# Layer 0 of a two-layer trunk: one forward substitution for both head groups, their inverses joined side by side, scan chunks of the groups in turn, and the output projection by token tile

## The chip, the core and the metric

The kernel runs on one core of a Trainium2 chip. The metric is the time of one execution on the device, in microseconds; what is compared is the median of several executions. The core has engines that each work through their own queue in order: PE (TensorE, the matmuls; PEld is its weight loads), DVE (VectorE), ACT (ScalarE), POOL (GpSimd), and SP, which here only issues DMAs. An instruction waits at the head of its queue until what it needs is there, and everything behind it on that engine waits too.

## What is computed

Two post-norm layers over 512 tokens of width 1024. Layer 0 mixes with a gated delta rule of six heads beside a cross-attention into 256 memory tokens, then comes an MLP of width 4096; layer 1 has sliding-window attention beside its own memory attention, then the same MLP. The part that matters here is the delta rule of layer 0:

```python
k_beta = k * beta[..., None]
L = jnp.where(strict, jnp.einsum('bhnid,bhnjd->bhnij', k_beta, k) * decay, 0.0)
rhs = jnp.concatenate([v * beta[..., None], k_beta * jnp.exp(g)[..., None]], axis=-1)
sol = lax.linalg.triangular_solve(L, rhs, left_side=True, lower=True, unit_diagonal=True)
...
def step(state, inp):
    qd, kd, uc, wc, ac, cd = inp
    v_new = uc - jnp.einsum('bhik,bhkv->bhiv', wc, state)
    out = jnp.einsum('bhik,bhkv->bhiv', qd, state) + jnp.einsum('bhij,bhjv->bhiv', ac, v_new)
    state = state * cd[..., None, None] + jnp.einsum('bhik,bhiv->bhkv', kd, v_new)
    return state, out
```

q, k and v pass a short causal convolution with SiLU first; the outputs are normed, gated by SiLU(z), joined with the memory attention and projected by w_o.

## The kernel before

Most matrix products are done in two parts: a weight tile `wr` arrives by DMA, ACT casts it to a rounded high part `wh` (L87) and DVE subtracts to get the low part `wl` (L88); three matmuls per tile then give the product. Three raw tiles and four pairs of parts are in flight in layer 0, so a new weight waits for the one four back to be used up. The six heads of the delta rule are two groups of three, and the 512 tokens are four chunks of 128, so a group has 12 units (head, chunk).

What is done in layer 0's mixer is written as a list of steps, `MIXER_ORDER`: a letter names a function, digits its arguments. `run_steps` calls them in that order; a scheduler then sets the queues of the engines, keeping to the order of the calls where operands allow and moving an instruction forward where its engine would stand. The steps are:

- `E` (`make_E1`): the decay matrices of a group, by a matmul over triangular masks (DVE and POOL build one each), DVE's mask and ACT's exponential. `g`, `k` (`group_kq`): k and q of one head: 48 matmuls, convolution (ACT one tap, DVE three: L324), SiLU, then `ak` (k with k and q), the norms, and the matrices LT (for the inverse) and INT (in the place of E).
- `i` (`inv_blocks`): the inverse of LT's diagonal 32x32 blocks. Four DMAs bring the blocks of a group's 12 units to 48 partitions (through DRAM, `dl`, then `ld`), 31 steps of forward substitution on DVE follow, a product (L420) and a subtraction (L422) each, and five DMAs bring the result back (`dx`, then the blocks of `TT`).
- `j` (`inv_join`): from these blocks to the whole 128x128 inverse. DVE transposes TT to U (L433); then small matmuls `ipp`, `ip3`, `ip2` (32x32) and, twice for six units, `iqp`, `iq2` (64x64), with ACT or DVE copying each result from PSUM for the next.
- `v` and `w`: v of one head (24 matmuls, convolution, SiLU), then its transposes (`vt`, L396) and scaling.
- `c` (`group_chunk`): one chunk of the scan for a group's three heads: transposes of k (`kt`), `ks` and `qs` with the state, DVE's subtraction R, `tr` with U, ACT's scaling to vn, `ds` for the new state and `od` for the output. `o` (`chunk_out`): the output's norm (ACT's squares, one power on POOL) and its product with the gate.
- `z` projects a third of the gate for all four token tiles; `n` (`z_norm`) applies SiLU (ACT) and the norm's weight (POOL, L625). `q` projects the memory queries; `m` (`mem0`) pushes a memory unit of a token tile: scores with exponentials, transposes (`mpt`), values (`mov`); a unit's later parts run when the next ones are pushed, and `M` flushes.
- `f` (`close_tile`) transposes a finished token tile to features (`to_feapt`), `W` loads a quarter of w_o, `p` projects a quarter for one tile, `L` is the layer norm of a tile, `X` closes the mixer's pool and opens those of the MLP.

Before, the first group's inverse is begun while the second group's heads are still projected, each group has its own substitution and its own join, the first group's four chunks come before the second's, and w_o is projected mostly after all tiles are closed. PSUM has eight banks: three for long products, five in turn for all small ones.

Of the kernel before, what the change touches and what calls it, by code (L numbers as in the profile page):

```python
# [18 lines left out]
P = 128  # L19
# [30 lines left out]
def trunk(ctx: ExitStack, tc: tile.TileContext, xT, xn, memT, wk, wq, wv, wqm, wz, wmk, wmv, wo0, wo1, up, dn,  # L50
# [24 lines left out]
    def fr(ap):  # L75
        return ap.bitcast(F32)
# [164 lines left out]

    def proj_z(zg, gates=None):

        slabs = [wload(wz[zg, kh], [P, 4, CW]) for kh in range(2)]
        c0 = zg * CW
        n = min(CW, 768 - c0)
        for t in range(NT):
# [7 lines left out]
    proj_z(2, ab)  # L255


# [45 lines left out]

    def make_E1(gi):
        E1 = dt_([P, NU, P], "E1")
        for hl in range(GH):
            h = GH * gi + hl
            ps = smt("E1")
            psv = ps.rearrange("p (c i) -> p c i", c=4)
            for i, eng in enumerate((V, G)):  # L310
                gm = dt_([P, 4, P], "y", dt=F32R)
                eng.tensor_tensor(gm, triu[:, :].unsqueeze(1).broadcast_to([P, 4, P]),
                                  fr(gsp[i])[:, h * 4:h * 4 + 4].unsqueeze(2).broadcast_to([P, 4, P]), op=ALU.mult)
                T.matmul(ps, slow, gm.rearrange("p c i -> p (c i)"), start=(i == 0), stop=(i == 1))
            dst = E1[:, hl * 4:hl * 4 + 4, :]
            V.tensor_tensor(dst, psv, mtri[:, :].unsqueeze(1).broadcast_to([P, 4, P]), op=ALU.add)
            A.activation(dst, dst, AF.Exp)
        E1s[gi] = E1

# [79 lines left out]

    Q = 4 * NU  # L400

    def inv_blocks(gi):

        LT = groups[gi]["LT"]
        dl = drp.tile([4, NU, 32, 32], F32, tag="dl", name=nm("dl"))
        for b in range(4):
            q = slice(32 * b, 32 * b + 32)
            SY.dma_start(dl[b].rearrange("u j i -> j u i"), LT[q, :, q])
        ld = dt_([Q, 32, 32], "ld", bufs=1)
        SY.dma_start(ld.rearrange("q j i -> q (j i)"), dl.rearrange("b u j i -> (b u) (j i)"))  # L410
        X = dt_([Q, 32, 32], "X", bufs=1)
        G.memset(X, 0.0)
        G.memset(X.rearrange("q i m -> q (i m)")[:, 0:1024:33], 1.0)
        tmp = dt_([Q, 256], "tmp", bufs=1)
        TT = groups[gi]["TT"] = dt_([P, NU, P], f"TT{gi}", bufs=1)
        G.memset(TT, 0.0)
        for j in range(31):
            n, m = 31 - j, j + 1
            tv = tmp[:, 0:n * m].rearrange("q (i m) -> q i m", m=m)
            V.tensor_tensor(tv, ld[:, j, j + 1:32].unsqueeze(2).broadcast_to([Q, n, m]),  # L420
                            X[:, j, 0:m].unsqueeze(1).broadcast_to([Q, n, m]), op=ALU.mult)
            V.tensor_sub(X[:, j + 1:32, 0:m], X[:, j + 1:32, 0:m], tv)  # L422
        dx = drp.tile([4, NU, 32, 32], F32, tag="dx", name=nm("dx"))
        SY.dma_start(dx.rearrange("b u i m -> (b u) (i m)"), X.rearrange("q i m -> q (i m)"))
        for b in range(4):
            q = slice(32 * b, 32 * b + 32)
            SY.dma_start(TT[q, :, q], dx[b].rearrange("u i m -> i u m"))

    def inv_join(gi):
        g = groups[gi]  # L430
        LT, TT = g["LT"], g["TT"]
        U = g["U"] = dt_([P, NU, P], "U")
        V.transpose(U.rearrange("p u i -> p (u i)"), TT.rearrange("p u i -> p (u i)"))  # L433

        b0, b1, b2, b3 = (slice(32 * b, 32 * b + 32) for b in range(4))
        pp = smt("ipp")[:, 0:NU * 32].rearrange("p (u i) -> p u i", u=NU)
        for u in range(NU):
            T.matmul(pp[b1, u, :], LT[b0, u, b1], TT[b0, u, b0], start=True, stop=True)
            T.matmul(pp[b3, u, :], LT[b2, u, b3], TT[b2, u, b2], start=True, stop=True)
        Pf = dt_([P, NU, 32], "Pf")  # L440
        A.copy(Pf[b1], pp[b1])
        V.tensor_copy(Pf[b3], pp[b3])
        p2 = smt("ip2")[:, 0:NU * 32].rearrange("p (u i) -> p u i", u=NU)
        p3 = smt("ip3")[:, 0:NU * 32].rearrange("p (u i) -> p u i", u=NU)
        for u in range(NU):
            T.matmul(p3[b1, u, :], U[b1, u, b1], Pf[b1, u, :], start=True, stop=True)
        for u in range(NU):
            T.matmul(p2[b0, u, :], Pf[b1, u, :], U[b1, u, b1], start=True, stop=True)
            T.matmul(p2[b2, u, :], Pf[b3, u, :], U[b3, u, b3], start=True, stop=True)
        V.tensor_scalar(TT[b1, :, b0], p3[b1], -1.0, None, op0=ALU.mult)  # L450
        A.activation(U[b0, :, b1], p2[b0], AF.Copy, scale=-1.0)
        V.tensor_scalar(U[b2, :, b3], p2[b2], -1.0, None, op0=ALU.mult)

        lo_, hi_ = slice(0, 64), slice(64, 128)
        for u0 in range(0, NU, 6):
            pp = smt("iqp")[:, 0:384].rearrange("p (u i) -> p u i", u=6)
            for u in range(6):
                T.matmul(pp[hi_, u, :], LT[lo_, u0 + u, hi_], TT[lo_, u0 + u, lo_], start=True, stop=True)
            P2 = dt_([P, 6, 64], "Pf")
# [282 lines left out]
    def second_pools():  # L742
# [6 lines left out]


    steps = {"E": make_E1, "g": group_open, "k": group_kq, "i": inv_blocks, "j": inv_join, "v": group_v,
             "w": group_v2, "c": group_chunk, "o": chunk_out, "q": proj_qm, "m": mem0, "M": flush, "z": proj_z,
             "n": z_norm, "W": wo_open, "f": close_tile, "p": wo_tile, "X": second_pools, "L": ln_tile}
# [528 lines left out]
```

## Time and profile before

| | us |
|---|---|
| median of 3 executions | 1174.53 (1172.65 to 1175.73) |
| the profiled execution | 1170.9 |
| its span, first to last instruction | 1169.2 |
| PE busy | 1137.7 (97%) |
| DVE busy | 860.7 (74%) |
| ACT busy | 555.8 (48%) |
| POOL busy | 242.5 (21%) |
| first z projection after the k and q heads | at 145.28 |
| first matmul of the MLP of layer 0 | at 325.71 |

The mean clock granted to PE is 0.992 of its full one. Times in rows of the timeline count from the first instruction. The mixer of layer 0 takes about the first 326 us; what follows, the two MLPs and layer 1, isn't touched by the change.

### The profile page before, as it was taken

What the parts mean: (1) busy time and instruction counts of PE and PEld (TensorE: products, weight loads), DVE (VectorE), ACT (ScalarE), POOL (GpSimd) and SP (SyncE); (2) the same over time, 40 slices, a digit from 0 to 9 for tenths busy, and PEclk for the clock granted to TensorE, in tenths of its full rate; (3) what the DMA queues carried; (4) which work ended last, traced back from release to release, by engine and by line L of the source; (5) the groups of instructions that cost most, each with busy time, mean ns of one, the idle gap of its engine ahead of it and who ended that gap; (6) DMA issues with size and microseconds to landing.
All of it is one profiled execution on the core that took longest, in us unless ns stands there. A gap on an engine that the chain in (4) does not pass through costs nothing.

```text
span 1169.2 us, 18962 instructions
## 1 busy us (share of the span) xinstructions
PE 1137.7 (97%) x7470; PEld 1000.1 (86%) x7470; DVE 860.7 (74%) x1606; ACT 555.8 (48%) x1010; POOL 242.5 (21%) x180
## 2 busy tenths in 40 slices
PE   8999999999999999999999999999999999999996
PEld 8877788879998989898998887778989998989985
DVE  5568899777798666667665968986987666676657
ACT  6345454655385434444443337562655344444431
POOL 1112111101005232423220100000042324242204
PEclk9999999999999999999999999999999999999998
DMA  7522141203413324232332242102333242323311
GB/s 257 194 63 77 61 137 37 68 20 105 166 57 127 124 75 139 76 125 92 100 117 92 71 129 71 54 21 72 109 118 118 77 140 73 126 91 105 112 37 72
DMA packets 40729, 114.16 MB, mean 98 GB/s; under 512 B 11136, under 2 KB 12032, under 8 KB 40640
## 3 DMA queue, kind: packets, MB, share of 16 engines
q1 hardware_dynamic: 40064, 112.04, 29.8%
q8 instruction: 58, 0.95, 0.3%
q10 hardware_dynamic: 576, 0.92, 0.2%
q14 instruction: 31, 0.25, 0.1%
HBM read 109.53 MB, written 3.41 MB: 97 GB/s over the span
## 4 chain that ended last, share of the span: by engine, by line
PE 76%; DVE 15%; ACT 3%; DMA 2%; issue 2%; POOL 1%; POOLq 0%; SPq 0%; ACTq 0%; DVEq 0%
PE dn L116 9%; PE dn L117 9%; PE dn L115 9%; PE upb L884 3%; PE upb L885 3%; PE upb L886 3%; PE wo L117 2%; DVE wl L88 2%; PE wo L115 2%; PE wo L116 2%; PE upd L885 2%; PE upd L884 2%; PE upd L886 2%; PE upa L885 2%; PE upa L884 2%; PE upa L886 2%
## 5 line engine op out<-in xcount | busy, mean ns | idle before, releaser
L87 ACT CAST wh<-wr 128x1024 fp32r<-128x1024 f32 (+1 forms) x136 | 142.6, 1052 | 221.9 <-PE dn L117 154.6
L88 DVE TENSOR_TENSOR wl<-wr,wh 128x1024 fp32r<-128x1024 f32 (+1 forms) x136 | 166.3, 1225 | 77.7 <-ACT wh L87 77.0
L115 PE MATMUL dn<-wh,hh 128*128 128x512 f32 x512 | 199.5, 390 | 0.0
L117 PE MATMUL dn<-wh,hl 128*128 128x512 f32 x512 | 199.4, 389 | 0.0
L116 PE MATMUL dn<-wl,hh 128*128 128x512 f32 x512 | 199.4, 389 | 0.0
L117 PEld LDWEIGHTS dn<-wh,hl 128*128 128x128 f32 x512 | 96.1, 188 | 20.1
L963 DVE TENSOR_TENSOR res<-res,dn 128x512 f32<-128x512 f32 x120 | 81.8, 682 | 42.4 <-PE dn L117 42.3
L116 PEld LDWEIGHTS dn<-wl,hh 128*128 128x128 f32 x512 | 96.1, 188 | 19.1
L115 PEld LDWEIGHTS dn<-wh,hh 128*128 128x128 f32 x512 | 96.1, 188 | 19.0
L874 POOL TENSOR_TENSOR sa<-wr 128x512 f32<-128x512 f32 x26 | 39.0, 1500 | 351.0 <-DMA wr<-in_up_dram 311.1
L662 POOL TENSOR_TENSOR rs<-rs,nhalf 128x1 f32<-128x1 f32 x16 | 13.3, 833 | 327.2 <-DVE rs L661 264.0
L884 PE MATMUL upb<-TH,wh 128*128 128x256 f32 x208 | 57.5, 277 | 1.5 <-DVE u L923 1.5
L885 PE MATMUL upa<-XL,wh 128*128 128x256 f32 x208 | 57.7, 277 | 0.0
L886 PE MATMUL upa<-XH,wl 128*128 128x256 f32 x208 | 57.5, 276 | 0.0
L122 DVE TENSOR_TENSOR hl<-r,hh 128x1024 fp32r<-128x1024 f32 x26 | 56.1, 2156 | 1.9 <-ACT hh L121 1.9
L885 PE MATMUL upb<-TL,wh 128*128 128x256 f32 x208 | 57.4, 276 | 0.0
L886 PE MATMUL upb<-TH,wl 128*128 128x256 f32 x208 | 57.4, 276 | 0.0
L884 PE MATMUL upd<-XH,wh 128*128 128x256 f32 x208 | 57.4, 276 | 0.0
L885 PE MATMUL upd<-XL,wh 128*128 128x256 f32 x208 | 57.4, 276 | 0.0
L886 PE MATMUL upd<-XH,wl 128*128 128x256 f32 x208 | 57.4, 276 | 0.0
L875 POOL TENSOR_TENSOR sb<-sa,wr 128x512 f32<-128x512 f32 x26 | 57.4, 2207 | 0.0
L121 ACT CAST wh<-wr 128x1024 fp32r<-128x1024 f32 x26 | 27.4, 1053 | 53.5 <-PE upa L885 53.5
(405 smaller groups left out, 3296.8 us busy)
## 6 DMA issues: line engine op xcount, KB each, us to landing
wr<-in_up_dram SPq DMA_DIRECT2D x64, 512.0 KB, 4.3
wr<-in_dn_dram SPq DMA_DIRECT2D x64, 512.0 KB, 4.3
wr<-in_wo_dram SPq DMA_DIRECT2D x16, 512.0 KB, 3.6
wr<-in_bw_dram SPq DMA_DIRECT2D x8, 512.0 KB, 4.5
wr<-in_wz_dram SPq DMA_DIRECT2D x6, 520.0 KB, 4.4
wr<-in_wk_dram SPq DMA_DIRECT2D x6, 512.0 KB, 3.6
wr<-in_wq_dram SPq DMA_DIRECT2D x6, 512.0 KB, 3.7
wr<-in_wv_dram SPq DMA_DIRECT2D x6, 512.0 KB, 3.6
```

The costliest lines, as they stand in the source:

```text
L87: A.copy(hi, raw)
L88: V.tensor_sub(lo, raw, fr(hi))
L115: T.matmul(ps, sh, hi[:, kk, :], start=(k == 0), stop=False)
L116: T.matmul(ps, sh, lo[:, kk, :], start=False, stop=False)
L117: T.matmul(ps, sl, hi[:, kk, :], start=False, stop=(k == nk - 1))
L122: return V.tensor_sub(lo, src, fr(hi))
L874: G.tensor_tensor(sa[:, 0], raw[1][:, kA], raw[1][:, kB], op=ALU.add)
L875: G.tensor_tensor(sb[:, 0], sa[:, 0], raw[0][:, kA], op=ALU.subtract)
L884: T.matmul(ps, hi[:, k, :], m, start=start and k == 0, stop=False, skip_group_check=True)
L885: T.matmul(ps, hi[:, k, :], ml[:, k, :], start=False, stop=False, skip_group_check=True)
L886: T.matmul(ps, lo[:, k, :], mh[:, k, :], start=False, stop=stop and k == 3, skip_group_check=True)
L963: V.tensor_tensor(dst, dst, ps, op=ALU.add)
```

## The change

The substitution is split off its DMAs: `i` now only gathers a group's blocks (`inv_gather`), to partitions 0 to 47 or 48 to 95 of one tile, and the new step `I` (`inv_blocks`) runs the 31 steps once on 96 partitions and sends both groups' blocks back. `j` has no argument any more: `inv_join` does each link for both groups before the next link. The chunks alternate between the groups. A memory unit's three parts are steps of their own (`m`, `t`, `u`), the decay matrices come head by head, `z` can be asked for single tiles, and w_o's first two quarters are projected as soon as a tile is closed.

```diff
-MIXER_ORDER = """q0 g1 g0 E0 k02 k01 k00 E1 k12 i0 k10 k11 q1 z1 m3 v00 i1 m1 w00 v01 j0 m0 v02 w01 m2 z0 w02 M c00 v10 n0 o00
-c01 n1 v11 w10 o01 c02 n2 o02 j1 c03 v12 w11 w12 c10 n3 W1 W0 o03 o10 c11 f0 o11 c12 o12 f1 W3 c13 p10 p00 o13
-p01 f3 f2 X p11 p02 p12 p03 W2 p23 p20 p30 p32 p31 L0 p21 p13 p22 L1 L2 p33 L3"""
+MIXER_ORDER = """q0 g1 g0 E02 E01 k02 E00 k01 E12 k00 E11 k12 i0 E10 k10 k11 i1 I q1 z1 z0 v00 v01 w00 v02 w01 w02 v10 j
+w10 v11 w11 v12 w12 W1 W0 c00 m0 c10 n0 o00 t0 o10 u0 c01 m1 c11 f0 n1 o01 t1 o11 u1 p10 c02 p00 f1 c12 m2 n2 o02 t2 o12 u2
+p11 c03 p01 f2 c13 m3 n3 o03 t3 o13 u3 p12 p02 f3 p13 p03 W3 X W2 p30 p31 p20 L0 p21 p32 L1 p22 p33 L2 p23 L3"""
...
-    def inv_blocks(gi):
-
+    def inv_gather(gi):
+
+        if not diag:
+            diag["ld"], diag["X"] = (dt_([P, 32, 32], n, bufs=1)[0:2 * Q] for n in ("ld", "X"))
+            G.memset(diag["X"], 0.0)
+            G.memset(diag["X"].rearrange("q i m -> q (i m)")[:, 0:1024:33], 1.0)
...
+        SY.dma_start(diag["ld"][gi * Q:gi * Q + Q].rearrange("q j i -> q (j i)"), dl.rearrange("b u j i -> (b u) (j i)"))
+
+    def inv_blocks():
...
+            V.tensor_tensor(tv, ld[:, j, j + 1:32].unsqueeze(2).broadcast_to([2 * Q, n, m]),
+                            X[:, j, 0:m].unsqueeze(1).broadcast_to([2 * Q, n, m]), op=ALU.mult)
             V.tensor_sub(X[:, j + 1:32, 0:m], X[:, j + 1:32, 0:m], tv)
...
-    def inv_join(gi):
+    def inv_join():
...
+        for g in gs_:
...
+            pp = smt("ipp")[:, 0:NU * 32].rearrange("p (u i) -> p u i", u=NU)
...
+        for g in gs_:
+            U, TT, Pf = g["U"], g["TT"], g["Pf"]
...
+        parts = [(g, u0) for g in gs_ for u0 in range(0, NU, 6)]
...
+        for (g, u0), P2 in zip(parts, prods):
             pp = smt("iqp")[:, 0:384].rearrange("p (u i) -> p u i", u=6)
...
+        for (g, u0), P2 in zip(parts, prods):
+            U = g["U"]
             p2 = smt("iq2")[:, 0:384].rearrange("p (u i) -> p u i", u=6)
...
-    def mem0(t):
-        push(mem_unit(dp, t, lambda j: res[:, t, 768 + j * P:768 + (j + 1) * P], KM[0], VM[0], res[:, t, :]))
+    mem_units = {}
+
+    def mem0(stage, t):
+        if stage == 0:
+            mem_units[t] = mem_unit(dp, t, lambda j: res[:, t, 768 + j * P:768 + (j + 1) * P], KM[0], VM[0], res[:, t, :])
+        mem_units[t][stage]()
```

Both programs have 7,038 matmuls, 888 instructions on ACT (13 of them loads of a function table) and 252 DMAs issued by SP; on DVE 1,608 instructions become 1,546. What moves is the order on each engine. Three places of it follow.

On PE, in the join, before: the second group's small products (`ipp`, `ip3` and `ip2`, here both printed `ip`), with v12's projection.

```order
L439 MATMUL ipp_2492<-TT_225_1719,LT_63_674 32x32
L107 MATMUL v_2621<-XH,wl_2625 128x512
L105 MATMUL v_2621<-XH,wh_2624 128x512
L106 MATMUL v_2621<-XL,wh_2624 128x512
L446 MATMUL ip_347_2521<-Pf_2517,U_2490 32x32 x12
L448 MATMUL ip_346_2520<-U_2490,Pf_2517 32x32
L107 MATMUL v_2621<-XH,wl_2625 128x512
```

On PE, in the join, now: both groups' 64x64 products (U_1954 and U_1984 are the two groups'), then three transposes of v and the first chunk's kt and tr.

```order
L475 MATMUL iqp_2098<-TT_194_1441,LT_72_683 64x64 x6
L475 MATMUL iqp_2106<-TT_194_1441,LT_72_683 64x64 x6
L475 MATMUL iqp_2114<-TT_195_1443,LT_63_674 64x64 x6
L475 MATMUL iqp_2122<-TT_195_1443,LT_63_674 64x64 x6
L481 MATMUL iq_266_2130<-U_1954,ld_2096 64x64 x6
L481 MATMUL iq_267_2138<-U_1954,ld_2096 64x64 x6
L481 MATMUL iq_268_2146<-U_1984,X_2097 64x64 x6
L481 MATMUL iq_269_2154<-U_1984,X_2097 64x64 x6
L399 MATMUL vt_2163<-ident,vt_1947 128x128 x4
L399 MATMUL vt_2207<-ident,vt_2200 128x128 x4
L499 MATMUL kt_2283<-ident,kq_675 128x128 x3
L516 MATMUL tr_2290<-vr_1859,U_1954 128x128 x3
```

The projections that stood between the links of a join now stand ahead of it, all of them; between the first `ipp` and the last `iq2` there is none left.

On DVE, in the substitution, now: its steps (`tmp`, `X`), the convolution of v00 (`y_1815`) and a weight of v11 (`wl`).

```order
L429 TENSOR_TENSOR tmp_1440<-ld_1187,X_1188 96x252
L88 TENSOR_TENSOR wl_2173<-wr_2170,wh_2172 128x1024
L431 TENSOR_TENSOR X_1188<-X_1188,tmp_1440 96x14x18
L327 SCALAR_TENSOR_TENSOR y_1815<-v_1783,convw,y_1815 128x511
L429 TENSOR_TENSOR tmp_1440<-ld_1187,X_1188 96x247
L327 SCALAR_TENSOR_TENSOR y_1815<-v_1783,convw,y_1815 128x510
L431 TENSOR_TENSOR X_1188<-X_1188,tmp_1440 96x13x19
L327 SCALAR_TENSOR_TENSOR y_1815<-v_1783,convw,y_1815 128x509
```

On PE, the transposes that need this y, now: after seven matmuls of v02 (`v_1866`), the rest of which stands behind them.

```order
L105 MATMUL v_1821<-XH,wh_1824 128x512
L106 MATMUL v_1821<-XL,wh_1824 128x512
L107 MATMUL v_1821<-XH,wl_1825 128x512
L105 MATMUL v_1866<-XH,wh_1869 128x512
...
L399 MATMUL vt_1860<-ident,vt_1814 128x128 x4
L106 MATMUL v_1866<-XL,wh_1869 128x512
```

The first y of v, and with it v00's transposes, stands behind 36 of the 62 steps; before, substitution steps and y alternated in the same way, in two substitutions of 48 partitions.

On ACT, at the first two chunks, now: kd, vn and the squares of the first group (LT_299), kd and vn of the second (LT_311), with the exponentials of memory unit 0 and the load of their table between.

```order
L518 ACTIVATE LT_299_2282<-tr_2290,brk_678 128x128 x3
L547 ACTIVATE junk_2353,sso_2352<-LT_299_2282 128x128 x3
L501 ACTIVATE LT_311_2325<-kt_2326,kds_671 128x128 x3
L518 ACTIVATE LT_311_2325<-tr_2333,brk_669 128x128
L579 ACT_TABLE_LOAD
L579 ACTIVATE p_2315,den_2314<-msc_2307,mx_2313 128x256 x2
L579 ACTIVATE p_2316,den_2314<-msc_2308,mx_2313 128x256 x2
L518 ACTIVATE LT_311_2325<-tr_2333,brk_669 128x128 x2
L591 COPY pT_2370<-mpt_2365 128x512
```

Before, the memory units stood among the v and z projections, ahead of the chunks; now they stand between the two groups' chunks.

More of the change, by code (lines that the diff above doesn't have):

```diff
@@ L240, in dt_, with proj_z @@
         return dp.tile(shape, dt, tag=tag, name=nm(tag), bufs=bufs)
-    def proj_z(zg, gates=None):
-        slabs = [wload(wz[zg, kh], [P, 4, CW]) for kh in range(2)]
+    z_slabs = {}
+    def proj_z(zg, *ts, gates=None):
+        if zg not in z_slabs:
+            z_slabs[zg] = [wload(wz[zg, kh], [P, 4, CW]) for kh in range(2)]
+        slabs = z_slabs[zg]
         c0 = zg * CW
         n = min(CW, 768 - c0)
-        for t in range(NT):
+        for t in ts or range(NT):
             ps = mmt("proj_zMM")
@@ L302, in trunk, with make_E1 @@
     NU = GH * 4
[L304 to L318, printed above, removed]
+    def make_E1(gi, hl):
+        if gi not in E1s:
+            E1s[gi] = dt_([P, NU, P], "E1")
+        h = GH * gi + hl
+        ps = smt("E1")
+        psv = ps.rearrange("p (c i) -> p c i", c=4)
+        for i, eng in enumerate((V, G)):
+            gm = dt_([P, 4, P], "y", dt=F32R)
+            eng.tensor_tensor(gm, triu[:, :].unsqueeze(1).broadcast_to([P, 4, P]),
+                              fr(gsp[i])[:, h * 4:h * 4 + 4].unsqueeze(2).broadcast_to([P, 4, P]), op=ALU.mult)
+            T.matmul(ps, slow, gm.rearrange("p c i -> p (c i)"), start=(i == 0), stop=(i == 1))
+        dst = E1s[gi][:, hl * 4:hl * 4 + 4, :]
+        V.tensor_tensor(dst, psv, mtri[:, :].unsqueeze(1).broadcast_to([P, 4, P]), op=ALU.add)
+        A.activation(dst, dst, AF.Exp)
     def conv_silu(ps, ch, dst):
@@ L408, in inv_blocks @@
             SY.dma_start(dl[b].rearrange("u j i -> j u i"), LT[q, :, q])
[L409 to L416, printed above, removed]
+        SY.dma_start(diag["ld"][gi * Q:gi * Q + Q].rearrange("q j i -> q (j i)"), dl.rearrange("b u j i -> (b u) (j i)"))
+    def inv_blocks():
+        ld, X = diag["ld"], diag["X"]
+        tmp = dt_([2 * Q, 256], "tmp", bufs=1)
+        for gi in range(2):
+            TT = groups[gi]["TT"] = dt_([P, NU, P], f"TT{gi}", bufs=1)
+            G.memset(TT, 0.0)
         for j in range(31):
@@ L424, in inv_blocks @@
[L424 to L427, printed above, removed]
-    def inv_join(gi):
[L430 to L433, printed above, removed]
-        b0, b1, b2, b3 = (slice(32 * b, 32 * b + 32) for b in range(4))
[L436 to L452, printed above, removed]
-        lo_, hi_ = slice(0, 64), slice(64, 128)
-        for u0 in range(0, NU, 6):
```

42 lines of the change are left out of this document (34 added, 8 removed).

## The prediction

> **What bounds the kernel now.** I read the page first, then windows of 20 us over layer 0's mixer, then the timeline of TensorE (PE). The windows' columns are stretch, length, and busy time (instructions) of PE, PEld, DVE, ACT and POOL, then PE's granted clock and the DMA share.
>
> ```profile
> span 1169.2 us, 18962 instructions
> ...
> 200.00:220.00 20.00, 17.17 (x100) 13.88 (x99) 18.81 (x39) 14.54 (x30) 4.20 (x3) 0.91 0.09 27
> ...
> 240.00:260.00 20.00, 18.08 (x236) 15.42 (x234) 13.49 (x33) 10.01 (x29) 1.70 (x2) 0.91 0.10 28
> 260.00:280.00 20.00, 18.78 (x149) 17.31 (x149) 14.26 (x48) 14.26 (x56) 3.39 (x4) 1.00 0.17 54
> 280.00:300.00 20.00, 20.00 (x174) 20.00 (x173) 12.61 (x27) 7.65 (x15) 0.85 (x1) 1.00 0.68 252
> ```
>
> PE is almost always "busy", even in the stretch that starts only 100 matmuls where a later one starts 174. Busy time hides the losses, because a record lasts longer than the step to the next one. The timeline shows the steps (start, duration, instruction):
>
> ```profile
> 145.28 0.36 PE L115 MATMUL proj_zMM<-wh,XH 128*128 128x260 f32 x1 [0.21 <-DVE y L324]
> ...
> 164.18 0.40 PE L106 MATMUL v<-XL,wh 128*128 128x512 f32 x1
> 164.41 0.39 PE L107 MATMUL v<-XH,wl 128*128 128x512 f32 x1
> ...
> 325.59 0.28 PE L117 MATMUL wo<-wh,XL 128*128 128x256 f32 x1
> 325.71 0.28 PE L105 MATMUL up<-XH,wh 128*128 128x256 f32 x1
> ```
>
> A 512-column matmul takes 0.23 us from start to start and a 256-column one 0.12, while their records last 0.40 and 0.28. So I give each record the median step of its line and form and call the rest **lost**. The first and last rows above bound the part that the change rebuilds: from the first z projection after the k and q heads to the MLP's first matmul, 180.4 us with 1,490 records. Their steps come to 162.2 us, so **18.2 us are lost**: 5.3 up to 213 us, 4.4 from there to 244, 1.8 in the second group's join (244.0 to 253.3), 6.3 in the following chunks and the closings (to 287.1), 0.4 after. The k and q heads before it (53.2 to 145.3) lose 6.4, and the MLP's first 19 us lose 2.1. The change adds and drops no matmul, so it can win at most these 27 us, 2.3%. Any wait that it makes PE meet counts in full.
>
> The worst wait of now is a model for the forecast:
>
> ```profile
> 212.10 1.85 POOL L625 TENSOR_TENSOR res<-res,nw_b 128x768 f32<-128x768 f32 x1 [2.41 <-ACT res L623]
> ...
> 212.55 1.57 DVE L420 TENSOR_TENSOR tmp<-ld,X 48x156 f32<-48x156 f32 x1
> ...
> 213.18 0.39 PE L105 MATMUL v<-XH,wh 128*128 128x512 f32 x1
> 214.05 0.73 DVE L324 SCALAR_TENSOR_TENSOR y<-v,convw,y 128x509 f32<-128x509 f32 x1
> ...
> 214.81 0.63 ACT L326 ACTIVATE vt<-y 128x512 f32<-128x512 f32 x1 [2.79 <-DVE y L324]
> ...
> 215.50 0.84 PE L396 MATMUL vt<-ident,vt 128*128 128x128 f32 x4 [1.93 <-ACT vt L326]
> ```
>
> PE stands in its queue before the transposes of a v head. They need the convolution's y, which on DVE alternates with substitution steps, one of them stretched to 1.57 us beside a GpSimd z norm.
>
> **The change, part by part.** *The substitution.* Groups of DVE rows over 60 to 330 us (busy us, mean ns):
>
> ```profile
> L88 DVE TENSOR_TENSOR wl<-wr,wh 128x1024 fp32r<-128x1024 f32 (+1 forms) x32 | 39.0, 1223 | 5.9 <-ACT wh L87 5.9
> L324 DVE SCALAR_TENSOR_TENSOR y<-v,convw,y 128x511 f32<-128x511 f32 (+2 forms) x18 | 13.3, 738 | 1.0 <-ACT y L322 0.9
> L420 DVE TENSOR_TENSOR tmp<-ld,X 48x31 f32<-48x31 f32 (+15 forms) x62 | 24.2, 390 | 0.8 <-POOL X L413 0.2
> L422 DVE TENSOR_TENSOR X<-X,tmp 48x31 f32<-48x31 f32 (+15 forms) x62 | 21.9, 354 | 0.6
> L433 DVE STREAM_TRANSPOSE U<-TT 128x1536 f32<-128x1536 f32 x2 | 3.5, 1766 | 0.0
> L442 DVE COPY Pf<-ipp 32x384 f32<-32x384 f32 x2 | 1.1, 564 | 0.8 <-ACT Pf L441 0.7
> L506 DVE COPY S<-ds 128x384 f32<-128x384 f32 x2 | 1.1, 550 | 0.0
> ```
>
> 62 of 124 steps go. 46.1 us of DVE fall to about 26, if 96 partitions cost what 48 do; the two 384-element copies say so (0.56 us on 32 partitions, 0.55 on 128). It is DVE time, worth only what PE waited for. Meetings with the four z norms stay:
>
> ```profile
> 190.55 1.83 POOL L625 TENSOR_TENSOR res<-res,nw_b 128x768 f32<-128x768 f32 x1 [18.03 <-ACT res L623]
> ...
> 190.56 2.10 DVE L420 TENSOR_TENSOR tmp<-ld,X 48x252 f32<-48x252 f32 x1
> ```
>
> 2.10 us instead of some 0.41; the four cost DVE 5.6 us. The Trainium skill, SBUF — State Buffer, section "SBUF: two separate sides", states an exclusive lock here: of a DVE instruction with two SBUF inputs and a GpSimd one that reads SBUF, the later waits for the whole of the other. Row and rule agree, and by the rule every norm still in flight during the only substitution stops it, as my sum has it.
>
> *k and q heads.* DVE no longer runs the first group's substitution among the second group's heads, and the E steps come one by one, with more table loads on ACT there. Bounds: nothing, or 4 of the 6.4 lost. I take **2 us won**, the middle: ak waits for y there, and y for DVE, but the new loads stand in ACT's part of the same chain.
>
> *From the heads to the join.* I walk the new rows with the old durations. PE's start stays at 145.3. The z projections and the last ak end at 170, v00 at 175.7, v01 at 181.3; after 7 more matmuls, at 182.9, PE stands before the transposes of v00. DVE meanwhile starts the substitution after v01's weights, whose buffers come free when z1 ends (159.3): two casts and two subtractions later, at 162. Up to v00's last y stand 36 steps (12.3 us of a whole of 20.3, with 0.03 between steps 1.1 more), three weight subtractions (3.4), the four norms (5.6), then two steps and three y (2.8): 187.2, and the silu (0.63) gives 187.9. PE waits **5.0 us**, then 0.9 and 0.3 for the next two heads. The norms' four passes fall together into 163 to 173 us. The substitution ends near 206, PE's projections at 211.5. Then come the DMAs:
>
> ```profile
> L424 SPq DMA_DIRECT2D dx<-X x2: 335/335/335, 167.1 to 223.5; - x2
> ...
> DMA to landing us min/median/max: 3.0/3.5/4.1
> ...
> L427 SPq DMA_DIRECT2D TT<-dx x8: 315/469/1087, 171.3 to 228.5; - x8
> ...
> DMA to landing us min/median/max: 2.2/2.4/2.8
> ```
>
> On SP, one wo load stands between dx and TT; its buffer is free by then. 3.5 us, then four issues of 0.47 and 2.4 us: the first group's blocks are there at 214. PE waits **2.5 us** more. Bounds of these waits together: 1 (norms elsewhere) to 12.
>
> *The join, side by side.* In the old order v and z matmuls stand between its links, so 1.8 us were lost. In the new one the only fill is the other group. Its links, with ACT's durations:
>
> ```profile
> L87 ACT CAST wh<-wr 128x1024 fp32r<-128x1024 f32 (+1 forms) x136 | 142.6, 1052 | 221.9 <-PE dn L117 154.6
> ...
> L561 ACT ACTIVATE p<-msc,mx 128x256 f32<-128x256 f32 x16 | 7.4, 473 | 0.0
> ...
> L500 ACT ACTIVATE LT<-tr,brk 128x128 f32<-128x128 f32 x24 | 7.1, 370 | 2.8 <-PE tr L498 2.7
> ...
> L561 ACT ACT_TABLE_LOAD x4 | 5.1, 1283 | 2.6 <-DVE mx L557 2.6
> ...
> L529 ACT ACTIVATE junk<-LT 128x128 f32<-128x128 f32 x24 | 7.5, 312 | 3.6 <-DVE LT L519 3.2
> ...
> L529 ACT ACTIVATION_READ_ACCUMULATOR junk<-LT 128x1 f32 x24 | 4.6, 192 | 0.0
> ```
>
> The first copy of ipp on DVE stands behind the last wo subtraction and v12's three y: v12 ends at 211.5, cast 1.05, subtraction 1.2, y 2.0, so 215.8. Then each group needs a copy (0.56), the transpose (1.77), ip3 (0.75 with its latency) and two negations (1.1): 8.4 us in DVE's order for both. iqp, its four ACT copies, iq2 and the negations take 5.6, v's transposes 1.3. From 214 to 232 are 18 us for 11.3 us of matmul: **7 us lost** (bounds 3 and 10).
>
> *Chunks.* The chain of waits gives what PE has to do there:
>
> ```profile
> 185.07 0.84 PE iqp L458 x12
> ...
> 205.83 1.75 PE mov L581 x16
> ...
> 274.21 0.87 PE to_feapt L613 x8
> 275.08 0.67 PE ks L490 x6
> ```
>
> Each of a chunk's six products is 0.67 us (the transposes 0.33), a memory unit 3.5, a closing 0.87. After the first chunk's vn, ACT holds in one queue its three squares (0.4 each with the accumulator), three kd (0.3), one vn, a table load (1.28), four exponentials (0.6 each), two vn: 7 us, and PE's ds, mpt and the second chunk stand behind them. Up to the second pair, 9.5 us of matmul take 15.4: **5.9 lost**. In the later pairs ACT needs 11.6 us a pair (six each of squares, kd, qs and vn, four exponentials, a copy, two casts) against 11.7 of PE, 17 with two wo tiles, so PE should be the bound; but each product still stands behind something in ACT's or DVE's queue: I get 2.4 at the second chunk of the second pair and a fifth of a microsecond to two at each later link, **8 us** in all. Bounds for both together: 0 (each chain hides the other) and 18.
>
> *The end.* W3 and W2 have 5.4 us of wo tiles before them and cost nothing; without that cover W2's 3.7 us load would show. The first layer norm stands 18 matmuls (2.0 us) after its tile, with 3.3 us of work: 1.3 lost; against it 1.5 of the MLP's first 2.1 go, since the other tiles come earlier.
>
> **The sum:** 5.0 + 1.2 + 2.5 + 7 + 5.9 + 8 = 29.6 lost where 18.2 were, 2 won at the heads, 0.2 at the end: 9.2 us more. The profiled execution took 1170.9 us, 0.3% under the median of 1174.53; so 1180 in its terms and **1183.5** in the median's. 0.3% (3.5 us) is what a measurement can tell.
>
> **The rivals.** *The two chains hide each other* (ends faster). If in the four chunk pairs PE never waits for ACT, the 13.9 us of the chunks go: 1169.6. It decides from a loss under 1.4 us there on. For it: the first group's chunks with v matmuls between ran well. Against: ACT's order above, one queue for both.
>
> *No meeting with the norms* (ends the same). If DVE is 5.6 us earlier and y is in time, 5.0 + 1.2 + 2.5 go: 1174.8. For it: the old first substitution, over by 167 us, met none, as the norms come at 190 and later. Against: now the norms become ready within the substitution's first 11 us.
>
> *The halved clock* (slower still).
>
> ```profile
> 214.70:218.10 3.40, 2.60 (x9) 2.22 (x10) 3.40 (x9) 3.26 (x8) 0.00 (x0) 0.67 0.27 61
> ```
>
> After the 1.93 us of wait at 213 the clock was cut for 3.4 us, and the window from 240, with the join in it, has a mean of 0.91 too. The new order has some six such stretches; at 1.0 to 1.7 us each, less two, 6 us: 1189.5. The Trainium skill, TensorE: Matmul & The Clock Gate, section "What's actually happening", asks for a whole idle window of some 3.4 us before the cut; by that the new order would have one or two and the sum would stay. The rows cut earlier than the page, so I keep the rival.
>
> *It doesn't do what it says:* were 96 partitions twice the price, 20 us of DVE would stand before the join: 1203. The two copies speak against it.
>
> **How the numbers follow.** Forecast (1179 to 1187) 0.41; halved clock 0.18; twice the price 0.02; hidden chains, below 1171.0, 0.22; no meeting, 0.17. Faster 0.22, same 0.17, slower 0.61. The range reaches from 1166 (the chains hidden and the heads' other 2 to 4 us) to 1193 (halved clock and the join's upper bound).
>
> **What would show it.** PE's rows before the v transposes: 4 to 6 us of wait for vt, DVE's y behind steps of 1.5 to 2.1 us. No v or z matmul between ipp and the last iq2, and 18 us from first ipp to first kt. ACT at a table load while ds waits. The forecast is wrong if the substitution is over before 200 us with y in time, or if the chunk pairs run without PE waiting for ACT; then the change is no loss.

## The result, and the profile after

| | before | after |
|---|---|---|
| median, us | 1175.05 (1172.65 to 1175.73, 4 runs) | 1190.08 (1186.08 to 1191.8, 4 runs) |
| ratio of after to before | | 1.0128, 95% interval 1.0102 to 1.0155 |
| profiled execution, us | 1170.9 | 1191.2 |
| its span, us | 1169.2 | 1189.5 |
| mean granted clock of PE | 0.992 | 0.979 |

The change makes the kernel 15.0 us slower (12.0 to 18.2 by the interval) where 9.2 were forecast. The two profiled executions differ by 20.3 us, since that of before lies 4.1 us under its median and that of after 1.1 over. The same kernel profiled once more on another chip had a span of 1185.1 us; readings below that rest on sizes are made on both.

The windows of 20 us over after's mixer; the columns are stretch, length, busy time (instructions) of PE, PEld, DVE, ACT and POOL, PE's granted clock, and the DMA share with GB/s:

```profile
200.00:220.00 20.00, 14.28 (x160) 11.72 (x160) 14.83 (x25) 6.34 (x9) 0.00 (x0) 0.89 0.46 119
220.00:240.00 20.00, 16.94 (x245) 16.33 (x242) 7.59 (x11) 3.96 (x8) 0.00 (x0) 0.50 0.01 2
240.00:260.00 20.00, 16.56 (x112) 14.81 (x112) 9.51 (x30) 11.63 (x43) 1.70 (x2) 0.84 0.00 1
260.00:280.00 20.00, 18.58 (x156) 17.45 (x154) 11.99 (x39) 11.87 (x47) 1.70 (x2) 1.00 0.09 27
```

The row that was not there before is the second: in 20 us PE works at half its clock, and DVE (7.6 us), ACT (4.0) and the DMAs are nearly idle. But for a wait of 3.3 us for DVE, the bound there is PE itself, with a chain of small matmuls at half pace.

The timeline of PE gives the stages (start, duration, instruction, in brackets the idle time before it and what ended it):

```profile
141.66 0.28 PE L115 MATMUL proj_zMM<-wh,XH 128*128 128x260 f32 x1
...
180.08 0.40 PE L105 MATMUL v<-XH,wh 128*128 128x512 f32 x1
186.65 0.69 PE L399 MATMUL vt<-ident,vt 128*128 128x128 f32 x2 [6.17 <-ACT vt L329]
...
213.00 0.22 PE L452 MATMUL ipp<-TT,LT 32*32 32x32 f32 x2 [1.97 <-DMA TT<-dx]
...
217.91 1.29 PE L462 MATMUL ip<-Pf,U 32*32 32x32 f32 x21 [3.43 <-DVE U L449]
...
239.96 0.63 PE L499 MATMUL kt<-ident,kq 128*128 128x128 f32 x2
...
348.33 0.29 PE L105 MATMUL up<-XH,wh 128*128 128x256 f32 x1
```

From the first z projection to the MLP's first matmul the part that the change rebuilds now takes 206.7 us instead of 180.4, for the same matmuls and eight transposes of a layer norm (0.9 us) that came after it before. The heads ahead of it are 3.6 us shorter (141.66 against 145.28). What is lost, counted as in the forecast (each step over its form's median, the small matmuls by the medians of before, since after's own are those of the half clock):

| stage of after, us | lost | forecast |
|---|---|---|
| heads, 53.2 to 141.7 | 2.8 (6.4 before) | 2 won |
| wait before v00's transposes, 180.1 to 186.6 | 6.3 | 5.0 |
| from there to the first ipp, 213.0 | 4.1: 2.1 before the blocks, 2.0 mostly in steps at half pace until 191.7, when a cut of the clock ends | 1.2 + 2.5 |
| join, 213.0 to 240.0 | 13.0: 6.8 in two waits, 6.2 in steps at half pace | 7 |
| chunks up to the second pair, to 260.5 | 7.6 | 5.9 |
| later chunks and closings, to 313.9 | 7.0 | 8 |
| w_o and layer norms, to 348.3 | 3.9 (0.3 before) | 1.3 |

The steps of the small matmuls are so short that the 6.2 depend on how their medians are taken, by a microsecond or two; a run below measures this part as 7.5. The two waits of the join are 3.6 us at 214.3 and 3.3 at 221.3, each for the copy and the transpose on DVE, less a step each. The pace can be read off the pairs of ipp, first of the first group (0.03 us from pair to pair), then of the second (0.05):

```profile
213.97 0.19 PE L453 MATMUL ipp<-TT,LT 32*32 32x32 f32 x1
213.97 0.19 PE L452 MATMUL ipp<-TT,LT 32*32 32x32 f32 x1
214.00 0.19 PE L453 MATMUL ipp<-TT,LT 32*32 32x32 f32 x1
...
220.74 0.24 PE L453 MATMUL ipp<-TT,LT 32*32 32x32 f32 x1
220.74 0.24 PE L452 MATMUL ipp<-TT,LT 32*32 32x32 f32 x1
220.79 0.24 PE L453 MATMUL ipp<-TT,LT 32*32 32x32 f32 x1
```

The substitution and its meetings with the z norms went as forecast. The groups of DVE rows (busy us, mean ns; idle before):

```profile
L431 DVE TENSOR_TENSOR X<-X,tmp 96x31 f32<-96x31 f32 (+15 forms) x31 | 15.1, 485 | 0.7
L429 DVE TENSOR_TENSOR tmp<-ld,X 96x31 f32<-96x31 f32 (+15 forms) x31 | 11.9, 384 | 2.0 <-DMA ld<-dl 1.4
```

In the timeline:

```profile
163.31 0.27 DVE L429 TENSOR_TENSOR tmp<-ld,X 96x112 f32<-96x112 f32 x1
163.38 1.91 POOL L643 TENSOR_TENSOR res<-res,nw_b 128x768 f32<-128x768 f32 x1 [0.99 <-ACT res L641]
163.61 1.80 DVE L431 TENSOR_TENSOR X<-X,tmp 96x112 f32<-96x112 f32 x1
```

The substitution takes 27.0 us on DVE where 46.1 stood (about 26 forecast). Between 160 and 172 four norms stretch a step each to some 1.8 us, as the step at 163.61 here; it ends at 205.7.

### The profile page after: what moved, and what is told of

It reads as the page before. It is cut to its first block, busy times and chain, and to the rows that moved or that the text cites. A ratio compares the mean times of both kernels' runs of the same rounds, so it can differ in the third digit from the quotient of the medians.

```text
span 1189.5 us, 18898 instructions
## 1 busy us (share of the span) xinstructions
PE 1146.3 (96%) x7470; PEld 1010.6 (85%) x7470; DVE 846.8 (71%) x1544; ACT 555.4 (47%) x1010; POOL 241.0 (20%) x178
## 4 chain that ended last, share of the span: by engine, by line
PE 85%; DVE 8%; ACT 3%; DMA 2%; issue 1%; POOL 1%; SPq 0%; POOLq 0%; DVEq 0%; ACTq 0%
PE dn L116 9%; PE dn L115 9%; PE dn L117 9%; PE upb L907 3%; PE upb L909 3%; PE upb L908 3%; PE upa L908 2%; PE upa L909 2%; PE upa L907 2%; PE upd L909 2%; PE upd L907 2%; PE upd L908 2%; DVE wl L88 2%; PE kq L105 2%; PE kq L106 2%; PE kq L107 2%
```

## The experiments

Theories: **chains** (the loss is PE's waits for DVE, ACT and DMA, as summed in the forecast), **clock** (the half clock in the join is a cost of its own), **cover** (what costs is that no wide projection is left to stand between the links of the join and the chunks). Chips and sessions differ by some microseconds (the medians of before are 1171.7 to 1175.1 us), so every run is given by its ratio to before on its own chip. The changed kernel, run again, had 1.0138.

> The changed kernel once more, unaltered, on the chip of the next runs, so that they are compared with it and not over two chips: 1.010 to 1.015 of the time of before.

Measured: 1.0138 (1.0113 to 1.0164). Its stages are those of the first profile: join 27.1 us with 13.1 lost, wait before v00 5.8.

### Added matmuls in the join's waits

```diff
+        bank = mmt("fill")
+        def fill(after, n):
+            with tc.issue_after(after.ins):
+                for i in range(n):
+                    last = T.matmul(bank, XH[:, i % KT, 0:P], XH[:, (i + 1) % KT, :], start=True, stop=True)
...
+            fill(last, 14 if g is gs_[0] else 12)
```

The edit also names v11 and v12 ahead of `j` and holds the second group's ipp behind the first group's products, so that the order of PE's other matmuls stays.

> 26 matmuls of 512 columns on values nobody reads are added on PE, 14 right behind the first group's ipp and 12 right behind the second group's, in the two waits of 3.6 and 3.3 us of the join; PE's other order stays. Clock theory (the half clock of 27 us is a cost of its own, set off because PE has no wide matmuls there): the clock in the join stays near 1.0, the join falls from 27 to about 20 or 21 us, the time falls by 6 to 8 us to about 1183. Chain theory (the join is as long as DVE's and ACT's links, the clock only shows it): the join stays at 27 us or grows by up to 1, the time is 1190 or 1191.

Measured: 1.0081 (1.0060 to 1.0102), some 6.7 us under the changed kernel (the two intervals don't meet), though PE does 26 matmuls more. The windows of this run, with the join in them:

```profile
210.00:215.00 5.00, 3.43 (x59) 2.57 (x58) 3.42 (x5) 2.18 (x4) 0.00 (x0) 1.00 0.55 95
215.00:220.00 5.00, 4.24 (x130) 3.57 (x128) 3.23 (x4) 0.70 (x2) 0.00 (x0) 1.00 0.02 3
220.00:225.00 5.00, 5.00 (x98) 4.23 (x97) 3.30 (x5) 0.73 (x2) 0.00 (x0) 1.00 0.01 3
225.00:230.00 5.00, 5.00 (x88) 4.93 (x87) 2.17 (x5) 1.90 (x4) 0.00 (x0) 1.00 0.00 0
```

The clock stays at 1.00 and the join takes 19.6 us instead of 27.1. The clock theory gave 20 to 21. The chains' part is still there, covered by matmuls that do nothing (6.0 us of them); the rest was the clock.

### The same on 32 rows and 32 columns

```diff
-                    last = T.matmul(bank, XH[:, i % KT, 0:P], XH[:, (i + 1) % KT, :], start=True, stop=True)
+                    last = T.matmul(bank[0:32], XH[0:32, i % KT, 0:32], XH[0:32, (i + 1) % KT, :], start=True, stop=True)
```

> As the run with 26 added matmuls in the join's two waits, at the same places and of the same number of columns (512), but on 32 rows and 32 columns of the array instead of 128 and 128. If the clock follows whether PE is busy at all: it stays near 1.0 and the join is near 20 us, as there, and the time about 1.008 of before. If a matmul on a sixteenth of the array counts as idle: the clock falls to 0.50 for the join as in the changed kernel, the added matmuls then overrun the two waits by 1 to 3 us, and the time is 1.013 to 1.017 of before.

Measured: 1.0180 (1.0158 to 1.0201), a little over what the second case gave. Windows over the two stretches of added matmuls, and one of iqp behind them:

```profile
212.00:217.50 5.50, 5.50 (x30) 2.21 (x24) 3.63 (x4) 0.47 (x1) 0.00 (x0) 0.56 0.01 3
222.00:227.00 5.00, 5.00 (x15) 1.80 (x14) 2.06 (x2) 0.19 (x1) 0.00 (x0) 0.50 0.00 0
230.00:235.00 5.00, 5.00 (x53) 5.00 (x52) 0.55 (x1) 1.64 (x4) 0.00 (x0) 0.50 0.00 0
```

PE is busy in every one of these 15.5 us and has about half its clock all the same. The cut begins at 212.6, 0.4 us after the first added matmul, and some 11 us of them do not lift it. So it is not PE's idling that the clock follows here: matmuls on a sixteenth of the array, however long, do not bring it back. Whether they would have held a full clock, this run doesn't show. The join grew to 31.5 us, since the 14 added matmuls took 5.8 us in a wait of 3.6 and the 12 took 5.3 in one of 3.3.

### The z norms behind the substitution

```diff
-        G.tensor_tensor(zv, zv, nw_b[:, :].unsqueeze(1).broadcast_to([P, NH, P]), op=ALU.mult)
+        zn = G.tensor_tensor(zv, zv, nw_b[:, :].unsqueeze(1).broadcast_to([P, NH, P]), op=ALU.mult)
+        tc.add_manual_dep(zn.ins, diag["last"].ins.name, ...)
```

> The four z norms on POOL wait for the last substitution step; no queue changes its order. If their meetings with the substitution are the price (5.6 us of DVE): DVE's y comes that much earlier, PE's wait of 6.3 us before v00's transposes falls to about 1 us, the half clock behind it (2 us) goes, the substitution ends near 200 instead of 205.7; the time falls by 7 to 9 us to about 1182. Rival, the meetings only move (DVE's weight subtractions and the join are slowed instead, or PE waits for the blocks what it gained): less than 3 us.

Measured: 1.0108 (1.0090 to 1.0127), 2 to 4 us under the changed kernel. The intervals overlap with its own, but on the same chip the MLP's first matmul comes 2.4 us earlier (343.1 against 345.5). The first half of the expectation came true: PE no longer waits before v00's transposes, the substitution ends at 199.0, the first ipp comes at 207.1. The second half did not. The timeline of DVE and POOL in this run:

```profile
199.12 8.20 POOL L643 TENSOR_TENSOR res<-res,nw_b 128x768 f32<-128x768 f32 x4 [47.55 <-DVE X L431]
...
199.63 2.42 DVE L88 TENSOR_TENSOR wl<-wr,wh 128x1024 fp32r<-128x1024 f32 x1 [0.66 <-ACT wh L87]
201.98 2.30 DVE L327 SCALAR_TENSOR_TENSOR y<-v,convw,y 128x511 f32<-128x511 f32 x3
205.97 2.43 DVE L88 TENSOR_TENSOR wl<-wr,wh 128x1024 fp32r<-128x1024 f32 x1 [1.69 <-ACT wh L87]
208.32 2.30 DVE L327 SCALAR_TENSOR_TENSOR y<-v,convw,y 128x511 f32<-128x511 f32 x3
210.65 0.56 DVE L456 COPY Pf<-ipp 32x384 f32<-32x384 f32 x1
```

The norms now meet the weight subtractions (2.42 us instead of 1.22), v12's y stands behind those, and the join's first copy behind that y. So the join's first wait grew from 3.6 to 4.8 us, that for the blocks from 2.1 to 2.9, and nearly all of the join runs at 0.50 again. The three y, which read PSUM and one SBUF input, take their usual 0.75 each. The Trainium skill, SBUF — State Buffer, section "SBUF: two separate sides", has an exclusive lock between a DVE instruction with two SBUF inputs and a GpSimd one that reads SBUF; these rows agree with it.

### The memory units ahead of the join

```diff
-... i1 I q1 z1 z0 v00 ... c00 m0 c10 n0 o00 t0 o10 u0 c01 m1 c11 ...
+... i1 I q1 z1 m0 m1 t0 t1 u0 m2 u1 t2 u2 z0 v00 ... c00 c10 n0 o00 o10 c01 c11 ...
```

> The first three memory units are done during the z projections instead of among the chunks, so that they cover PE's wait for y and leave v projections for the join. If ACT's queue with the table load and the exponentials is what PE waits for in the first chunks: the 7.6 us lost there fall to 4 or less, PE's waits before v00's transposes (6.3) mostly go, the projections left in the join keep its clock up; the time falls by 10 to 15 us to about 1177. Rival: the units' work on DVE (7.8 us) delays the substitution by as much, PE waits for the blocks instead, and the time is within 4 us of 1190.

Measured: 1.0057 (1.0038 to 1.0076), 8 to 10 us under the changed kernel, short of the 10 to 15. PE's wait before v00's transposes fell from 6.3 to 2.2 us, but the units bring 2.7 us of new waits among the z projections. The chunks gain next to nothing: up to the second pair they lose 7.1 us as before (7.6), though no memory unit and no table load is among them any more. Most of the gain lies in the join, in which 48 v matmuls are now left: 5.6 us lost instead of 13.0, with the clock at 1.00 from 210 to 230. Of the 5.6, 5.1 stand in front of the last head's transposes (timeline):

```profile
233.12 0.40 PE L107 MATMUL v<-XH,wl 128*128 128x512 f32 x1
238.62 1.11 PE L399 MATMUL vt<-ident,vt 128*128 128x128 f32 x4 [5.11 <-ACT vt L329]
```

> Both the late norms and the early memory units. If their gains add up: 15 to 22 us, at 1168 to 1175, as fast as the kernel before or faster. If with the early memory units PE no longer waits for DVE ahead of the join, the norms are worth under 3 us here.

Measured with both edits: 1.0057 (1.0034 to 1.0079). By the medians they do not add up. In the two profiles PE has the same order from the z projections to the MLP, with the same 48 v matmuls in the join, and here y is in time and the first ipp comes 2.0 us earlier, at 206.8. Yet the join loses 11.7 us: the clock is cut from 223.2 to 236.8, in the middle of it, where with the memory units alone the cut began at 236.3, in the wait before the last transposes:

```profile
220.00:230.00 10.00, 10.00 (x145) 8.99 (x143) 4.13 (x8) 2.37 (x6) 0.00 (x0) 0.66 0.03 8
230.00:240.00 10.00, 7.64 (x41) 6.46 (x39) 4.48 (x7) 2.34 (x3) 0.00 (x0) 0.66 0.00 0
```

So the order alone does not settle whether the clock is cut there. Of this kernel's ten executions six, the profiled one among them, took 1179.4 to 1181.4 us at a mean granted clock of 0.985 to 0.987, and four took 1172.6 to 1176.2 at 0.991 to 0.993; with the memory units alone seven of nine had such a clock, at 1175.5 to 1179.2. The means of these four and seven, 1174.3 and 1176.9, would fit norms worth under 3 us, hidden by the cut; no trace of the four is kept, so this is not shown.

> As the run with the memory units ahead, but the first group's first two chunks come before the transposes of the last v head, so that this head's convolution has cover. Fill theory: the wait of 5.3 us before those transposes goes, 3 to 6 us under that run, at 1.001 to 1.003 of before. Rival (the chunks' links wait for ACT and DVE whatever stands beside them): the wait turns up inside the chunks, within 2 us of that run.

Its edit is again in `MIXER_ORDER` alone: `... v11 w11 v12 W1 W0 c00 n0 o00 c01 n1 o01 w12 c10 ...`. Measured: 1.0050 (1.0031 to 1.0069), no better; by its time the rival was right. In the profile the 5.1 us went, and 4.2 us turned up before the first closing, whose transposes now wait for the second group's output. That execution is the longest of ten (1183.9 us, median 1177.4), with a cut of the clock from 252.9 to 263.1, so whether the others lose the time at this place is open.

### The groups' chunks one after the other

```diff
-... c00 m0 c10 n0 o00 t0 o10 u0 c01 m1 c11 f0 ...
+... c00 m0 n0 o00 t0 u0 c01 m1 n1 o01 t1 u1 c02 ... c03 m3 n3 o03 t3 u3 c10 o10 c11 f0 ...
```

> The changed kernel with the second group's chunks after the first group's instead of in turn. If the two chains cover each other in the changed kernel, the chunks lose 8 to 15 us more than their 14.6 now, and the time rises to about 1200. If each link waits for ACT's queue anyway, whichever group is next, the time stays within 3 us of the changed kernel's.

Measured: 1.0346 (1.0312 to 1.0380), 24 us over the changed kernel. The chunks lose 33.7 us instead of 13.1, and the clock falls with them:

```profile
260.00:280.00 20.00, 16.80 (x93) 14.34 (x93) 7.91 (x25) 8.29 (x33) 1.47 (x2) 0.74 0.00 1
280.00:300.00 20.00, 17.17 (x90) 14.69 (x90) 7.03 (x21) 8.47 (x34) 0.85 (x1) 0.74 0.00 0
```

Part of it is the memory units. One's transposes now follow its scores with no other group's chunk between, and before them PE waits for the exponentials 3.5, 2.2, 2.2 and 1.8 us; in the changed kernel there is one such wait, of 1.6. The first of the four (timeline):

```profile
243.09 1.14 PE L569 MATMUL msc<-KM,res 64*128 64x256 f32 x8
247.73 2.06 PE L587 MATMUL mpt<-ident,p 128*128 128x128 f32 x8 [3.51 <-ACT p L579]
```

The closings and w_o's projections also move behind the first group's chunks. So this run does not price the alternation of the scan's links alone. Taking the groups in turn is worth much in the new order, more than was expected; it replaces a good part of the cover that v's projections gave in the old.

### The single substitution alone

```diff
 # inv_join(gi) for one group, as before
-q1 z1 z0 v00 v01 w00 v02 w01 w02 v10 j w10 v11 w11 v12 w12 W1 W0 c00 m0 c10 ...
+q1 z1 m3 v00 m1 t3 w00 v01 m0 t1 u3 v02 w01 m2 t0 u1 z0 w02 t2 u0 u2 j0 c00 v10 n0 o00 c01 n1 v11 w10 o01 c02 n2 o02 j1 c03 v12 ...
```

> The single substitution and the new order of the heads alone: the joins of the two groups, the chunks, the memory units and w_o's projections come in the old order, so that v and z matmuls stand between the links again. Fill theory (what costs is that wide matmuls no longer stand between the links of the join and the chunks): the clock stays near 1.0, the heads' 3.6 us stay won, the time is 2 to 7 us under that of before (0.994 to 0.998). Rival (the single substitution itself costs, since the first group's inverse comes some 38 us later than of old): PE runs out of work ahead of the first join, and the time is 3 to 10 us over that of before.

Measured: 0.9967 (0.9954 to 0.9979), 3.9 us faster than before. The rival, too late a first inverse, falls: PE has 0.1 us of wait before the first ipp at 208.8. In the profiles this kernel is 2.6 us ahead of before at the MLP's first matmul, and 2.1 of that are won at the heads (143.2 against 145.3). The windows:

```profile
210.00:220.00 10.00, 10.00 (x156) 7.61 (x154) 8.03 (x9) 3.44 (x6) 0.00 (x0) 1.00 0.35 107
220.00:230.00 10.00, 10.00 (x89) 8.78 (x88) 6.65 (x12) 5.76 (x18) 0.00 (x0) 1.00 0.17 54
...
240.00:250.00 10.00, 8.09 (x121) 7.43 (x122) 6.95 (x15) 3.88 (x12) 0.85 (x1) 0.56 0.01 2
```

The first join (208.8 to 223.7) has v matmuls between its links and loses 0.6 us; the first group's first three chunks lose 0.8. The second join, from 238.4, has one v matmul left, gets half the clock from 241.2 to 254.9, against the expectation, and the window from 240 to 260 loses 7.5.

### Projections kept for the second join

```diff
+                if k == 4:
+                    tc.add_manual_dep(mms[0].ins, g["pin"].ins.name, ...)
```

`pin` is the second group's last ipp, `mms` v12's matmuls of one k.

> As the run with the single substitution in the old order, but the last 12 of v12's 24 matmuls (2.8 us) stand behind the second group's ipp, so that the second join has wide matmuls again. Clock theory: of the 7.5 us lost between 240 and 260 in that run, 2 to 4 go, and the chunks before it lose 1 or 2: 1 to 3 us faster than that run, 0.994 to 0.996 of before. Rival (the cover is only moved from the chunks to the join): within 1 us of that run, 0.997.

Measured: 0.9947 (0.9928 to 0.9967), 6.2 us faster than before, the lowest ratio of all. The 2.4 us between it and the run above are in the expected range, but not clear of the noise: the two intervals overlap. The second join has its clock, and loses 1.3 us; the first three chunks lose 2.6, and the first join, with a cut of its own, 2.1:

```profile
220.00:230.00 10.00, 9.54 (x69) 7.56 (x69) 5.68 (x7) 5.27 (x12) 0.00 (x0) 0.84 0.17 55
...
240.00:250.00 10.00, 9.24 (x182) 7.43 (x181) 6.44 (x18) 5.67 (x15) 0.85 (x1) 1.00 0.01 3
```

> The same with all 24 of v12's matmuls (5.5 us) behind the second group's ipp. Clock theory: the second join loses 4 us less, but the first group's chunks stand without cover and may have their own cut: between 0.993 and 0.997 of before. Rival (cover only moved): 0.997 to 1.000.

Measured with `k == 0`: 0.9995 (0.9981 to 1.0009). The clock is 1.00 in the second join, but v12 now ends at 251.1, and PE stands 4.8 us before its transposes. The time is in the rival's range. Cover must be kept, but not the projection whose result is needed next.

| run | ratio to before | 95% interval |
|---|---|---|
| changed kernel, first comparison | 1.0128 | 1.0102 to 1.0155 |
| again, with the next ones | 1.0138 | 1.0113 to 1.0164 |
| added wide matmuls | 1.0081 | 1.0060 to 1.0102 |
| added narrow matmuls | 1.0180 | 1.0158 to 1.0201 |
| late norms | 1.0108 | 1.0090 to 1.0127 |
| early memory units | 1.0057 | 1.0038 to 1.0076 |
| both | 1.0057 | 1.0034 to 1.0079 |
| early memory units, chunks before v12's transposes | 1.0050 | 1.0031 to 1.0069 |
| groups one after the other | 1.0346 | 1.0312 to 1.0380 |
| single substitution alone | 0.9967 | 0.9954 to 0.9979 |
| with 12 of v12's matmuls kept back | 0.9947 | 0.9928 to 0.9967 |
| with 24 | 0.9995 | 0.9981 to 1.0009 |

## Why the prediction was right, and where it was short

The direction was right, and the time lies in the range, but above the 1179 to 1187 of the forecast itself; the size was short by 5.8 us.

- **The substitution.** 96 partitions cost what 48 do: 27.0 us against the 26 of the forecast. The rival of twice the price falls.
- **The heads.** 3.6 us won instead of 2. The later runs with the same order of heads have their first z projection between 141.3 and 144.1, so the size stays loose; of before there is one profile.
- **The wait before v00's transposes.** 6.3 us (5.8 in the second profile) against 5.0, by the mechanism of the forecast: y on DVE among substitution steps, four of them stretched by norms. The late norms confirm that the meetings make this wait, and correct the rival *no meeting with the norms*: without them the kernel is some 2 us faster at the MLP, not 9, since the norms then meet what stands before the join.
- **The blocks.** 2.1 us against 2.5, at 213.0 against 214.
- **The join.** This is the step that failed: "18 us for 11.3 of matmul: 7 us lost". Its waits were sized right, 6.8 us. But the 11.3 us were counted at full pace, and PE got half its clock from 215.6 to 242.9: 6.2 us more by the table. The added matmuls show that this is a cost of its own: the clock stays at 1.00, and 7.5 us of the join go. What is left, 19.6 us, is 1.6 over the forecast's 18: the matmuls were also counted short, 11.3 us where the table leaves 27.0 - 13.0 = 14.0. (The forecast's own terms, 215.8 + 8.4 + 5.6 + 1.3, end at 231.1 and not at 232.)
- **The rival of the halved clock** gave 1189.5, near the time that came, but by luck: it had the right resource with the wrong pattern, six short cuts after waits, where there was one of 27 us, which narrow matmuls did not lift. Of the two signs that it names in before's trace, the cut in the window from 240 lies at 253.4 to 256.8, behind the second join and not in it. Beside the long cut stood two shorter ones, of 6.8 us from 184.9 on, in the wait for y, and of 3.4 us near 251. The forecast should have priced the join's own steps with and without the clock.
- **The chunks.** 14.6 us lost against 13.9, but the cause was named too narrowly. ACT does stand at a table load while mpt waits for its exponentials, as the rows below show. Yet without memory units and table load the first pairs lost about as much (7.1 us), and in the old order, with v matmuls between them, the first group's three chunks lost 0.8. What counts is cover, and each link's own length when there is none. The rival that the chains hide each other was wrong as an end (13 to 15 us are still lost) and right as a mechanism: 20 us more are lost without the alternation, 8 of them in waits for the memory units' exponentials.

The timeline of ACT and PE in after's second chunk:

```profile
246.89 0.38 ACT L518 ACTIVATE LT<-tr,brk 128x128 f32<-128x128 f32 x1
247.29 1.28 ACT L579 ACT_TABLE_LOAD   x1
247.32 0.49 PE L522 MATMUL ds<-LT 128*128 128x128 f32 x2 [0.79 <-ACT LT L518]
...
248.58 0.47 ACT L579 ACTIVATE p<-msc,mx 128x256 f32<-128x256 f32 x1
...
249.66 1.60 PE L587 MATMUL mpt<-ident,p 128*128 128x128 f32 x6 [1.62 <-ACT p L579]
```

- **The end.** Before the MLP 3.9 us are lost where 0.3 were, mostly 0.4 to 1.0 before each layer norm's transposes and in w_o's projections, and the MLP up to its first `dn` is 2.1 us shorter, 0.9 of it for the eight transposes that now come before it: 2.4 us worse, not 0.2 better. No run was spent on it.

By the medians: 15.0 us less the 6.7 that the added matmuls take back are 8.3, and the forecast, which knew all but the clock, had 9.2. That this comes so near is partly luck: the other terms were off by up to 2.6 us, in both directions.

## What to carry to other kernels

A stretch that chains small matmuls needs wide ones in its waits, to cover them and, apart from that, to hold PE's clock: before joining two such chains side by side, ask what wide work is left to stand there. Saved DVE time is worth what PE waited for; here the single substitution, with the heads' new order, gave 3.9 us with the old order around it, 6.2 with twelve projections kept back, and a loss with the new order. And where the clock can be cut, one profile is one draw: hold its clock against that of the other executions before explaining where the time went.

## What the runs showed of the hardware

In these runs the granted clock follows how much of the array works, not whether PE is busy. In after's join, with almost nothing but 32x32 and 64x64 matmuls, it was 0.50 for 27 us, 15 of them (225 to 240) without a gap on PE; with 26 matmuls of 128x128 and 512 columns added it was 1.00; with the same number on 32x32 0.50 again. In the run of the single substitution alone the clock fell at 241.2 although no wait in the 15 us before was over 0.7 us.

Narrow matmuls do not always bring a cut, though. The join's last 168 matmuls, all 32x32 or 64x64, took 12.5 us at 0.50 in after; in the run with added wide matmuls the same 168 took 6.9 us at 1.00. These are the two windows, after first:

```profile
224.60:237.10 12.50, 12.48 (x168) 12.38 (x168) 2.75 (x5) 2.38 (x5) 0.00 (x0) 0.50 0.01 2
222.80:229.70 6.90, 6.90 (x168) 6.79 (x165) 2.76 (x5) 2.38 (x5) 0.00 (x0) 1.00 0.01 2
```

They differ in the clock that the 168 began with. In after the cut stood already, made in the first wait; the narrow matmuls did not lift it, and it ended only after the 128x128 transposes at the join's end (237.2 on), at 242.9. With the added matmuls in the waits no cut came there.

Within the mixer each cut in the traces lasts 3.4 us or a multiple of it: 6.8, 10.2, 13.7, 27.3, 30.7. Whether one comes is not settled by PE's order: the run of the single substitution alone and that with 12 matmuls kept back have the same 644 matmuls in the same order from the first z projection into the first chunk, and only the second has a cut there, from 219.9 to 223.3.

The Trainium skill, TensorE: Matmul & The Clock Gate, section "What's actually happening", tells of an idle window of about 3.4 us before the cut and of a busy one before the clock returns. The cuts here agree with it only if a window of narrow matmuls can count as an idle one, and the 6.9 us show that it need not; the fraction of the array from which it counts as busy was not tried.

The windows of the 15 us in after's join:

```profile
225.00:230.00 5.00, 5.00 (x96) 4.94 (x94) 1.10 (x2) 1.00 (x3) 0.00 (x0) 0.50 0.02 3
230.00:235.00 5.00, 5.00 (x53) 5.00 (x52) 0.84 (x2) 1.38 (x3) 0.00 (x0) 0.50 0.00 0
235.00:240.00 5.00, 5.00 (x34) 4.56 (x34) 2.75 (x5) 0.63 (x1) 0.00 (x0) 0.50 0.01 2
```

The column of the clock, not that of PE's busy time, shows such a stretch.
